# Input projection of a two-layer hybrid decoder: chunk pairs over all tokens by Strassen's seven products, and the layer in two phases

## The chip, the core and the metric

The program runs on one core of one Trainium2 chip. The time is device microseconds of one execution. TensorE (PE) multiplies, VectorE (DVE) and ScalarE (ACT) do elementwise work, GpSimd (POOL) and SyncE (SP) mostly issue DMAs; each engine works through its own queue in order. Matrix products write to PSUM, in banks of 128 partitions x 512 float32 columns.

## The reference

Two layers over 1024 tokens of width 1024. In each layer a conditioning vector gives a shift, a scale and a gate, and one wide projection feeds three token mixers:

```python
u    = x * (1.0 + scale) + shift
proj = u @ w_in                      # (1024 tokens, 7840 columns)
# A: a1 * sigmoid(a2) -> causal depthwise conv of 31 taps -> LayerNorm -> silu, times silu(a_gate), @ w_a_out
# B: gb * conv3(gc * xb), times silu(b_gate), @ w_b_out
# C: attention of 8 heads with low-rank q and kv and a rotary part, times silu(c_gate), @ w_c_out
m    = sum(sigmoid(merge_i) * y_i for i in range(3))
x    = layer_norm(alpha * x + gate * (m @ w_o))
```

Everything is float32.

## The kernel before

Data lie with features on the 128 partitions and tokens along the columns. The program works in four windows: two layers, and in each the tokens 0 to 511 and 512 to 1023. A product keeps float32 precision by splitting each operand into two float32r parts (`split`: the high part by ACT, the low part by DVE) and adding three passes, high x high, high x low and low x high (L131 to L133). The columns of w_in make 61 chunks of 128; a chunk of a window is 8 row blocks x 3 passes = 24 matmuls into one of three PSUM banks of the tag "pj". Its weights come as two units of 128x512: SP loads one, ACT and DVE split it (L81, L82). This happens anew in each window. `run` loads the units LOOKAHEAD = 3 ahead.

The order of the work is a list of jobs in `build`, woven by hand (`weave` spreads one list evenly behind another); each engine's queue follows from it through the tile framework's scheduler, and waits between engines are put in by that framework. In a window come the latent chunks for attention (5), branch A's eight chunks, the up-projections, then the chunks of B, the gates and the first merge logits, woven with the attention (per head and block of 128 queries: scores into one two-bank PSUM tile, DVE's maximum at L673, ACT's exponential at L675, transposes at L691, values at L707). The 31 convolution steps on DVE (L521, 128x512 each, two channel blocks per job) are woven into the same stretch. Then follow the other merges and the product with w_o, and the layer norm of a window lies in the head of the next.

A merge logit is a chunk whose tanh (L756) is used at once. Branch outputs stay in SBUF. Between the windows only a few carried columns are copied on POOL (L499, L502, L602, L605), and q, k and v go through DRAM by DMAs of POOL's queue. POOL's only arithmetic on two tiles is at the very end (L888). The conditioning's weighted sums (L230) are on DVE.

## Time and profile before

| | |
|---|---|
| time, median of 3 runs (lowest, highest) | 2230.21 us (2229.93, 2230.97) |
| the profiled execution, first to last instruction | 2231.9 us |
| matmuls | 10635 |
| DMA traffic | 313.79 MB, mean 141 GB/s |
| window-wise loads of w_in | 488 of 256 KB |

The profile records one execution, from its first to its last instruction; what lies around that span is not in it, and the profiled execution's own time is taken as its span. Busy time of an engine is the union of its instructions. Matmuls overlap in the records (a 512-column one lasts 0.39 us there and the next starts before it ends), so their pace is read from the starts. "A <- B" names who ended a wait.

### The profile page before, as it was taken

The numbers are of one execution on the slowest core, as the hardware profiler recorded it, in microseconds if no ns is written. First come the engines' busy times: TensorE is split into PE (matmuls) and PEld (weight loads), VectorE is DVE, ScalarE is ACT, GpSimd is POOL, SyncE is SP. The second block draws the span as 40 slices with busy tenths as digits, with TensorE's granted clock in tenths as the row PEclk, the third lists the DMA queues.
The fourth block names the chain that finished last, engine by engine and source line by source line (L and its number), as shares of the span: only waits on it lengthen the run. The fifth ranks groups of instructions, "written<-read, shape, count | busy, mean of one in ns | idle before, by whom it ended". The sixth has DMA issues, their size and how long they took to land.

```text
span 2231.9 us, 30546 instructions
## 1 busy us (share of the span) xinstructions
PE 2188.0 (98%) x10635; PEld 1809.1 (81%) x10635; DVE 1680.6 (75%) x2899; ACT 1072.3 (48%) x1915; POOL 222.8 (10%) x443
## 2 busy tenths in 40 slices
PE   6999999999999999999999999999999999999995
PEld 5788888888888888888888888888888888888885
DVE  7999955667999976576689996465579999556555
ACT  3644453444636555343464445443455555554343
POOL 0121100000121210000003111000002121100000
PEclk9999999999999999999999999999999999999998
DMA  8584443345594564345549443233448655322331
GB/s 291 183 234 114 112 126 94 95 133 193 161 278 109 128 140 126 117 131 162 161 137 289 131 119 100 85 95 95 139 135 260 165 123 121 94 76 87 103 124 60
DMA packets 177066, 313.79 MB, mean 141 GB/s; under 512 B 19600, under 2 KB 51856, under 8 KB 176912
## 3 DMA queue, kind: packets, MB, share of 16 engines
q1 hardware_dynamic: 130640, 231.60, 34.0%
q0 software_dynamic: 46272, 80.24, 14.3%
q8 instruction: 84, 1.38, 0.3%
q14 instruction: 70, 0.57, 0.1%
HBM read 271.39 MB, written 40.37 MB: 140 GB/s over the span
## 4 chain that ended last, share of the span: by engine, by line
PE 85%; issue 10%; DVE 2%; ACT 1%; DMA 0%; POOL 0%; SPq 0%; POOLq 0%; ACTq 0%; DVEq 0%
PE lgps L131 7%; PE lgps L133 7%; PE lgps L132 7%; PE avps L707 3%; PE yps L131 3%; PE yps L133 3%; PE yps L132 3%; PE tps L691 3%; PE ops L132 2%; PE ops L131 2%; PE ops L133 2%; PE score L668 2%; PE score L669 2%; PE score L670 2%; PE latps L131 1%
## 5 line engine op out<-in xcount | busy, mean ns | idle before, releaser
L82 DVE TENSOR_TENSOR wsplit<-wraw,wsplit 128x512 fp32r<-128x512 f32 (+1 forms) x692 | 471.4, 683 | 239.0 <-ACT wsplit L81 235.6
L81 ACT CAST wsplit<-wraw 128x512 fp32r<-128x512 f32 (+1 forms) x692 | 424.8, 615 | 460.4 <-PE lgps L133 82.9
L521 DVE SCALAR_TENSOR_TENSOR cacc<-abuf,vec,cacc 128x512 f32<-128x512 f32 x480 | 341.9, 744 | 0.1
L131 PE MATMUL lgps<-u,wsplit 128*128 128x512 f32 x768 | 307.4, 400 | 0.0
L133 PE MATMUL lgps<-u,wsplit 128*128 128x512 f32 x768 | 300.0, 391 | 0.0
L132 PE MATMUL lgps<-u,wsplit 128*128 128x512 f32 x768 | 299.8, 390 | 0.0
L133 PEld LDWEIGHTS lgps<-u,wsplit 128*128 128x128 f32 x768 | 144.2, 188 | 31.1
L131 PEld LDWEIGHTS lgps<-u,wsplit 128*128 128x128 f32 x768 | 144.7, 188 | 27.1 <-issue 1.0
L132 PEld LDWEIGHTS lgps<-u,wsplit 128*128 128x128 f32 x768 | 144.5, 188 | 27.2 <-issue 1.0
L675 ACT ACTIVATE prob<-score,nm 128x384 f32<-128x384 f32 (+7 forms) x128 | 95.1, 743 | 124.8 <-DVE nm L673 117.2
L82 DVE TENSOR_TENSOR pt<-tps,pt 128x512 fp32r<-128x512 f32 (+1 forms) x160 | 101.5, 634 | 48.1 <-ACT pt L81 47.0
L756 ACT ACTIVATE mt<-lgps 128x512 f32<-128x512 f32 x96 | 57.4, 597 | 150.0 <-PE lgps L133 150.0
L81 ACT CAST pt<-tps 128x512 fp32r<-128x512 f32 (+1 forms) x160 | 86.4, 540 | 70.5 <-PE avps L707 61.4
L131 PE MATMUL ops<-m,wsplit 128*128 128x512 f32 (+1 forms) x320 | 111.2, 348 | 0.1
L132 PE MATMUL ops<-m,wsplit 128*128 128x512 f32 (+1 forms) x320 | 110.9, 347 | 0.0
L133 PE MATMUL ops<-m,wsplit 128*128 128x512 f32 (+1 forms) x320 | 110.7, 347 | 0.0
L673 DVE TENSOR_REDUCE nm<-score 128x1 f32<-128x384 f32 (+7 forms) x128 | 96.4, 753 | 15.5 <-PE score L671 14.4
L677 ACT ACTIVATE prob<-prob,nm 128x384 f32<-128x384 f32 (+7 forms) x128 | 99.5, 778 | 15.3 <-DVE nm L676 15.2
L707 PE MATMUL avps<-pt,Vh 128*128 128x256 f32 x640 | 104.9, 286 | 0.0
L707 PEld LDWEIGHTS avps<-pt,Vh 128*128 128x128 f32 x640 | 95.3, 189 | 10.4
L691 PE MATMUL tps<-cs,prob 128*128 128x128 f32 x576 | 89.7, 272 | 0.0
L691 PEld LDWEIGHTS tps<-cs,prob 128*128 128x128 f32 x576 | 71.9, 140 | 18.2
(306 smaller groups left out, 5029.3 us busy)
## 6 DMA issues: line engine op xcount, KB each, us to landing
wraw<-in_win SPq DMA_DIRECT2D x488, 256.0 KB, 2.7
wraw<-in_wout SPq DMA_DIRECT2D x96, 256.0 KB, 2.6
adaraw<-in_wada SPq DMA_DIRECT2D x64, 256.0 KB, 3.3
wraw<-in_wo SPq DMA_DIRECT2D x64, 256.0 KB, 2.8
Kh<-knD POOLq DMA_DIRECT2D x48, 256.0 KB, 4.7
Vh<-vD POOLq DMA_DIRECT2D x48, 256.0 KB, 4.1
adaraw<-in_wada SPq DMA_DIRECT2D x16, 512.0 KB, 6.7
knD<-knope POOLq DMA_DIRECT2D x16, 512.0 KB, 4.9
```

Source lines behind the costliest of these rows:

```text
L81: nc.scalar.copy(dst[:, 0], src)
L82: nc.vector.tensor_tensor(dst[:, 1], src, dst[:, 0].bitcast(F32), op=ALU.subtract)
L131: mm(ps, w[:, 0, c], x[k][:, 0, cols], start=k == 0, stop=False)
L132: mm(ps, w[:, 0, c], x[k][:, 1, cols], start=False, stop=False)
L133: mm(ps, w[:, 1, c], x[k][:, 0, cols], start=False, stop=k == 4 * len(units) - 1)
L521: nc.vector.scalar_tensor_tensor(acc, a[:, k:k + T], w, acc, op0=ALU.mult, op1=ALU.add)
L673: nc.vector.tensor_reduce(nm[:, 0:1], sp[:, :nk], axis=AX.X, op=ALU.max, negate=True)
L675: nc.scalar.activation(p[:, :nk], sp[:, :nk], AF.Exp, bias=nm[:, 0:1], accum_out=nm[:, 1:2])
L677: nc.scalar.mul(p[:, :nk], p[:, :nk], nm[:, 2:3])
L691: nc.tensor.transpose(tp[:, c:c + P], st["p", hd, 2 * half + b][:, (2 * kp + k) * P:(2 * kp + k + 1) * P], self.ident)
L707: mm(av[:, half * 256:(half + 1) * 256], v[:, 2 * kp + k], pt[:, w, (1 - k) * 256:(2 - k) * 256], start=kp == 0 and k == 0 and w == 0, sto ...
L756: nc.scalar.activation(st["t"], ps, AF.Tanh, scale=0.5)
```

## The change

56 of the 61 chunks are now computed in pairs, for all 1024 tokens at once. A pair is a 2x2 block product: two chunks by two halves of the 1024 input features, times two halves of the features by two halves of the tokens. Strassen's scheme (in Winograd's form) takes seven block products where eight stood. The factors on the side of u (X11, X12, X22 and the sums S1 to S4) are built once a layer and kept split in SBUF (`s_job`); those on the side of w_in are built for each pair by four subtractions on POOL (`pair_units`), and all seven factors are split by ACT and DVE. Each product adds into one of the three banks (A and C take two products, B three), and the sums across banks are made by one copy on ACT and five additions on DVE, which read the bank between two products (`pair_jobs`). The even row blocks of w_in come first in DRAM (KO). The latents (5 chunks) stay as they were.

A layer has two phases. The first computes the latents and up-projections for both halves of the tokens, then all 28 pairs: 12 of merge logits, 4 of A (a2, a1), 8 of B, 2 of C's gates and 2 of A's gates. The convolution runs over 1024 columns at a time, one channel block per job, woven into 12 of these pairs. The tanh of the logits, C's gates and the split branch outputs of A and B go to DRAM (by ACT's, POOL's and POOL's queue). The second phase does, for each half of the tokens, the merges with B and A woven with the attention (for the second half also w_o and the norm of the first), then the merges with C; logits are loaded on SP and branch outputs on POOL. SBUF tiles have fixed homes that serve several uses (HOMES).

```diff
-LOOKAHEAD = 3
-UPW = 20
-# bounds of the first units of weights, loaded behind each early block of the conditioning
-SP = (0, 3, 7, 10, 14)
+LOOKAHEAD = 5
+KO = (0, 2, 4, 6, 1, 3, 5, 7)
+SP = (0, 3, 6, 8, 10)
...
+    "X11": homes(0, 4), "S2": homes(4, 8), "S1": homes(8, 12), "X12": homes(12, 16), "S3": homes(16, 20),
+    "S4": homes(20, 24), "X22": homes(24, 28), "X21": ["c0", "c1", "c2", "c3"],
...
+    def pair_units(self, l, c1, c2):
+        nc = self.nc
+        st = {}
+        def raw(key, c, half):
+            st[key] = self.pw.tile([P, T], F32, tag="wr", name="wraw")
+            nc.sync.dma_start(st[key], self.win[l, c, :, half * T:(half + 1) * T])
+        def part(t):
+            w = self.pw.tile([P, 2, T], F32R, tag="ws", name="wsplit")
+            self.split(w, t)
+            return w
+        def minus(d, a, b):
+            nc.gpsimd.tensor_tensor(d, a, b, op=ALU.subtract)
+        def w11():
+            for key, c, half in (("11", c1, 0), ("12", c2, 0), ("22", c2, 1), ("21", c1, 1)):
+                raw(key, c, half)
+            return part(st["11"])
+        def t2():
+            minus(st["11"], st["12"], st["11"])
+            st["t2"] = self.pw.tile([P, T], F32, tag="tt", name="wt")
+            minus(st["t2"], st["22"], st["11"])
+            return part(st["t2"])
+        def t3():
+            minus(st["12"], st["22"], st["12"])
+            return part(st["12"])
+        def t4():
+            minus(st["t2"], st["21"], st["t2"])
+            return part(st["t2"])
+        return [w11, t2, lambda: part(st["11"]), lambda: part(st["21"]), t3, lambda: part(st["22"]), t4]
...
+    def pair_jobs(self, l, c1, c2, post, name):
+        nc = self.nc
+        st = {}
+        add = lambda d, a, b: nc.vector.tensor_tensor(d, a, b, op=ALU.add)
+        def tmp(key):
+            st[key] = self.t2("w", key)
+            return st[key]
+        def p1():
+            nc.scalar.copy(tmp("a1"), st["A"])
+        def p6():
+            add(tmp("a2"), st["a1"], st["B"])
+        def p5():
+            add(tmp("a5"), st["a1"], st["C"])
+        def p2():
+            post(0, 0, st["A"])
+        def p7():
+            add(st["a5"], st["a5"], st["B"])
+            post(1, 1, st["a5"])
+        def p3():
+            add(st["a2"], st["a2"], st["C"])
+            post(1, 0, st["a2"])
+        def p4():
+            add(st["a1"], st["a1"], st["B"])
+            post(0, 1, st["a1"])
+        steps = [("X11", "A", p1), ("S2", "B", p6), ("S1", "C", p5), ("X12", "A", p2), ("S3", "B", p7),
+                 ("S4", "C", p3), ("X22", "B", p4)]
+        units = self.pair_units(l, c1, c2)
+        def part(n, half):
+            key, b, end = steps[n]
+            def fn(ws):
+                if half == 0:
+                    st["w"] = ws[0]
+                    if n < 3:
+                        st[b] = self.bank(name, "pj")
+                w, ps = st["w"], st[b]
+                mm = nc.tensor.matmul
+                for k in (2 * half, 2 * half + 1):
+                    x = self.state[key, l][k]
+                    c = slice(k * P, (k + 1) * P)
+                    for i, (a, e) in enumerate(((0, 0), (0, 1), (1, 0))):
+                        mm(ps, w[:, a, c], x[:, e], start=n < 3 and k == 0 and i == 0, stop=k == 3 and i == 2,
+                           skip_group_check=True)
+                if half:
+                    end()
+            return ([] if half else [units[n]], fn)
+        return [part(n, half) for n in range(7) for half in range(2)]
...
+    def s_job(self, l, i):
+        nc = self.nc
+        x11, x12, x21, x22 = (self.affine(l, h, 2 * i + e, act=True) for h in range(2) for e in range(2))
+        tt = nc.vector.tensor_tensor
+        tt(x11, x11, x21, op=ALU.subtract)
+        self.factor(l, "S3", x11)
+        tt(x21, x21, x22, op=ALU.add)
+        self.factor(l, "S1", x21)
+        tt(x22, x22, x11, op=ALU.subtract)
+        self.factor(l, "S2", x22)
+        tt(x12, x12, x22, op=ALU.subtract)
+        self.factor(l, "S4", x12)
...
-    def conv_jobs(self, l, j0):
+                nc.scalar.activation(t, t, AF.Tanh, scale=0.5)
+                glu(1, t, st["v"])
+        return self.pair_jobs(l, CH_A2 + j, CH_A1 + j, post, "aps")
+    def conv_jobs(self, l, j):
         nc = self.nc
 
         def step(k):
             def fn(_):
-                for j in (j0, j0 + 1):
-                    w = self.vec[l][:, V_CAW + j * 31 + k:V_CAW + j * 31 + k + 1]
-                    a = self.state["abuf", j]
-                    if k == 0:
-                        acc = self.pt.tile([P, T + 30], F32, tag="ab", name="cacc")[:, :T]
-                        self.state["cacc", j] = acc
-                        nc.vector.tensor_scalar(acc, a[:, 0:T], w, self.vec[l][:, V_CAB + j:V_CAB + j + 1],
-                                                op0=ALU.mult, op1=ALU.add)
-                    else:
-                        acc = self.state["cacc", j]
-                        nc.vector.scalar_tensor_tensor(acc, a[:, k:k + T], w, acc, op0=ALU.mult, op1=ALU.add)
+                w = self.vec[l][:, V_CAW + j * 31 + k:V_CAW + j * 31 + k + 1]
+                a = self.state["abuf", j]
+                if k == 0:
+                    acc = self.pa.tile([P, S], F32, tag=f"c{j}", name="cacc")
+                    self.state["cacc", j] = acc
+                    nc.vector.tensor_scalar(acc, a[:, 0:S], w, self.vec[l][:, V_CAB + j:V_CAB + j + 1],
+                                            op0=ALU.mult, op1=ALU.add)
+                else:
+                    acc = self.state["cacc", j]
+                    nc.vector.scalar_tensor_tensor(acc, a[:, k:k + S], w, acc, op0=ALU.mult, op1=ALU.add)
...
+    def keep(self, key, t, scale):
+        p = self.pair("sp", "yp")
+        self.split(p, t, scale)
+        d = self.pd.tile([P, 2, T], F32R, name="y" + "".join(map(str, key)))
+        self.nc.gpsimd.dma_start(d, p)
+        self.state[("yD",) + key] = d
...
+    def logit_pair(self, l, n, d0):
+        nc = self.nc
+        def post(i, h, t):
+            key = ("tD", l, n, d0 + i)
+            if key not in self.state:
+                self.state[key] = self.pd.tile([P, S], F32, name=f"tD{l}{n}{d0 + i}")
+            m = self.t2("w", "mt") if (i, h) == (0, 0) else t
+            nc.scalar.activation(m, t, AF.Tanh, scale=0.5)
+            nc.scalar.dma_start(self.state[key][:, h * T:(h + 1) * T], m)
+        return self.pair_jobs(l, CH_M + 3 * d0 + n, CH_M + 3 * d0 + 3 + n, post, "lgps")
...
-        def logit(ps):
-            st["t"] = self.t2("m", "mt")
-            nc.scalar.activation(st["t"], ps, AF.Tanh, scale=0.5)
+        def logit(_):
+            st["t"] = self.t2("w", "mt")
+            nc.sync.dma_start(st["t"], self.state["tD", l, n, d][:, h * T:(h + 1) * T])
...
+            jobs += weave(part0, side0, 0, len(part0))
+            lat1, up1 = self.head(l, 1)
+            jobs += weave(lat1, [([], lambda _, l=l, i=i: self.s_job(l, i)) for i in range(4)], 2, len(lat1) - 2)
+            lg = [self.logit_pair(l, n, 2 * i) for n in range(3) for i in range(4)]
+            body = weave(lg[0] + lg[1], up1, 0, 28)
+            convs = [self.conv_jobs(l, j) for j in range(4)]
+            fill = [lg[2] + lg[3] + lg[4], lg[5] + lg[6] + lg[7], lg[8] + lg[9] + lg[10],
+                    lg[11] + self.cg_pair(l, 0) + self.cg_pair(l, 2)]
             for j in range(4):
-                fill += self.b_jobs(l, h, j)
-                if j % 2 == 0:
-                    fill += self.cg_job(l, h, j // 2)
-            for d in range(8):
-                fill += self.merge_jobs(l, h, "B", d)
-                if d % 4 == 1:
-                    fill += self.cg_job(l, h, 2 + d // 4)
-            body = weave(fill, self.att_jobs(l, h), 8, len(fill))
-            for d in range(8):
-                body += self.merge_jobs(l, h, "C", d)
-            lna = self.lna_jobs(l)
-            body = weave(body, self.conv_jobs(l, 0) + self.conv_jobs(l, 2) + lna[:2], 0, len(body) - 28)
-            body = weave(body, lna[2:], len(body) - 24, len(body) - 10)
-            tail = [j for k in range(4) for j in self.ag_job(l, h, k)]
-            for d in range(8):
-                tail += self.merge_jobs(l, h, "A", d)
-            last = w + 1 == len(wins)
+                body += self.a_pair(l, j) + weave(fill[j], convs[j], 0, len(fill[j]))
+            tail = [x for j in range(4) for x in self.b_pairs(l, j)]
+            lna = self.lna_jobs(l, 0) + self.lna_jobs(l, 1)
+            body += weave(tail, lna, 20, len(tail) - 14)
+            body += self.ag_pair(l, 0) + self.ag_pair(l, 2)
+            if l == 0:
+                body = weave(body, adas, 40, len(body) - 40)
+            jobs += body
+            for h in range(2):
+                ab = self.y_jobs(l, h, "B")
+                for d in range(8):
+                    ab += self.merge_jobs(l, h, "B", d)
+                ab += self.y_jobs(l, h, "A")
+                for d in range(8):
+                    ab += self.merge_jobs(l, h, "A", d)
+                if h:
+                    wo = [j for e in range(8) for j in self.wo_jobs(l, 0, e)]
+                    ab = wo + self.ln_jobs(l, 0) + ab
+                body = weave(ab, self.att_jobs(l, h), 0, len(ab) - 6)
+                for d in range(8):
+                    body += self.merge_jobs(l, h, "C", d)
+                jobs += body
```

## Rows read from the trace of the kernel before

**Rows 1.** The page: busy us (share of the span) and instructions of three engines.

```profile
span 2231.9 us, 30546 instructions
PE 2188.0 (98%) x10635; PEld 1809.1 (81%) x10635; DVE 1680.6 (75%) x2899; ACT 1072.3 (48%) x1915; POOL 222.8 (10%) x443
```

**Rows 2.** The page: the chain that ended last, shares by engine.

```profile
PE 85%; issue 10%; DVE 2%; ACT 1%; DMA 0%; POOL 0%; SPq 0%; POOLq 0%; ACTq 0%; DVEq 0%
```

**Rows 3.** Waits of PE: us in total, times, longest us.

```profile
PE adaps L238 <- DVE adacc L230: 14.9, 3, 11.6
```

**Rows 4.** Timeline of PE, 51 products in a row: start us, us.

```profile
400.21 0.39 PE L131 MATMUL lgps<-u,wsplit 128*128 128x512 f32 x1
...
411.55 0.39 PE L133 MATMUL lgps<-u,wsplit 128*128 128x512 f32 x1
```

**Rows 5.** Busy us (instructions) by stretch, then granted clock, DMA share, GB/s.

```profile
core 0: us, PE busy (x) PEld busy (x) DVE busy (x) ACT busy (x) POOL busy (x), PEclk, DMA share, GB/s
120.00:180.00 60.00, 60.00 (x280) 48.72 (x280) 58.82 (x104) 27.27 (x57) 16.21 (x33) 1.00 0.68 192
```

**Rows 6.** Timeline of DVE.

```profile
1327.92 0.75 DVE L521 SCALAR_TENSOR_TENSOR cacc<-abuf,vec,cacc 128x512 f32<-128x512 f32 x1
1328.58 0.69 DVE L603 TENSOR_TENSOR pbuf<-gcps,xb 128x512 f32<-128x512 f32 x1
1329.18 0.68 DVE L82 TENSOR_TENSOR wsplit<-wraw,wsplit 128x512 fp32r<-128x512 f32 x1
1329.78 0.48 DVE L608 TENSOR_SCALAR cvb<-pbuf,vec 128x512 f32<-128x512 f32 x1
```

**Rows 7.** DVE's groups by shape: busy us, mean ns | idle before.

```profile
L673 DVE TENSOR_REDUCE nm<-score 128x1 f32<-128x1024 f32 x16 | 19.6, 1222 | 4.0 <-PE score L671 3.5
...
L673 DVE TENSOR_REDUCE nm<-score 128x1 f32<-128x512 f32 x16 | 11.0, 686 | 1.1 <-PE score L671 1.0
...
L673 DVE TENSOR_REDUCE nm<-score 128x1 f32<-128x128 f32 x16 | 4.6, 286 | 0.7 <-PE score L671 0.7
```

**Rows 8.** Line 888: duration ns min/median/max, first and last start us.

```profile
L888 DVE TENSOR_TENSOR r<-r,emr x5: 411/420/504, 2218.1 to 2221.2; 128x256 f32<-128x256 f32 x5
...
L888 POOL TENSOR_TENSOR r<-r,emr x3: 723/727/781, 2218.4 to 2222.0; 128x256 f32<-128x256 f32 x3
L888 POOLq MODIFY_POOL_CONFIG  x2: 1/3/5, 2002.4 to 2002.4; - x2
```

**Rows 9.** Timeline near the end, DVE and POOL.

```profile
2220.30 0.72 POOL L888 TENSOR_TENSOR r<-r,emr 128x256 f32<-128x256 f32 x1 [1.16 <-DVE r L887]
2220.80 0.84 DVE L888 TENSOR_TENSOR r<-r,emr 128x256 f32<-128x256 f32 x2
```

**Rows 10.** Line 602, a copy of two columns on POOL.

```profile
L602 POOL COPY pbuf<-carryB x8: 185/197/634, 496.7 to 1830.4; 128x2 f32<-128x2 f32 x8
```

**Rows 11.** Timeline of POOL beside rows 6.

```profile
1329.33 0.58 POOL L605 COPY carryB<-pbuf 128x2 f32<-128x2 f32 x1 [5.50 <-DVE pbuf L603]
```

**Rows 12.** Busy us of a tile's own instructions: transposes, values, scores of one window.

```profile
140.00:360.00 220.00, 12.65 (x80) 10.22 (x80) 14.36 (x24) 12.33 (x24) 1.00 0.44 120
...
140.00:360.00 220.00, 15.25 (x96) 14.69 (x96) 5.46 (x8) 4.65 (x8) 1.00 0.44 120
...
140.00:360.00 220.00, 23.31 (x128) 16.67 (x96) 15.54 (x32) 19.81 (x64) 1.00 0.44 120
```

**Rows 13.** ACT's groups by shape.

```profile
L675 ACT ACTIVATION_READ_ACCUMULATOR prob<-score,nm 128x1 f32 x128 | 24.7, 193 | 0.0
...
L675 ACT ACTIVATE prob<-score,nm 128x512 f32<-128x512 f32 x16 | 11.0, 689 | 17.9 <-DVE nm L673 17.9
...
L675 ACT ACTIVATE prob<-score,nm 128x128 f32<-128x128 f32 x16 | 5.9, 368 | 11.5 <-DVE nm L673 11.5
```

**Rows 14.** Busy us of the start.

```profile
0.00:48.00 48.00, 28.89 (x125) 23.06 (x125) 35.33 (x67) 17.60 (x28) 0.30 (x5) 0.98 0.86 303
```

More of the change, by code (lines that the diff above doesn't have):

```diff
@@ L113, in run, with chunk @@
             fn(loaded[done - len(us):done])
[L115 removed]
+    def chunk(self, units, xs, post, name, tag="pj", cols=slice(0, T), kept=None, where=lambda k: (k // 4, k % 4)):
         st = {}
         kept = {} if kept is None else kept
[L119 removed]
+        again = "planned" in kept
+        kept["planned"] = True
+        n = 4 * len(units)
+        loaded = set()
         def part(i):
+            new = [] if again else sorted({where(k)[0] for k in (2 * i, 2 * i + 1)} - loaded)
+            loaded.update(new)
             def fn(ws):
@@ L137, in chunk @@
-        jobs = [part(i) for i in range(2 * len(units))]
-        kept.setdefault("planned", True)
-        return jobs
+            return ([units[u] for u in new], fn)
+        return [part(i) for i in range(n // 2)]
     def in_chunk(self, l, h, ch, post, name, tag="pj"):
         return self.chunk([self.win[l, ch, :, 0:T], self.win[l, ch, :, T:2 * T]],
-                          lambda: self.state["u", l, h], post, name, tag)
+                          lambda: self.state["u", l, h], post, name, tag, where=lambda k: (k % 2, k // 2))
@@ L916, in build @@
                         self.setup()
-                    for k in order[SP[n]:SP[n + 1]]:
-                        first[k] = self.load_w(units[k], "ws" if k < 4 else "br" if k < 12 else "PT")
+                    for k in range(SP[n], SP[n + 1]):
+                        first.append(self.load_w((units[k], HOMES["first"][k])))
                     self.u_job(0, 0, 2 * n)
@@ L970, in build @@
-            jobs += head + body + tail + wo
-            prev = (l, h)
-        jobs.append(([], lambda _: self.end_jobs(*prev, slice(T // 2, T))))
+                    part = [j for e in range(8) for j in self.wo_jobs(l, 1, e, c, tags[2 * e:2 * e + 2], kept[e])]
+                    jobs += weave(part, self.ln_jobs(l, 1, slice(0, T // 2)), 2, 30) if c.start else part
+        jobs.append(([], lambda _: self.end_jobs(L - 1, 1, slice(T // 2, T))))
         self.run(jobs, first)
```

366 lines of the change are left out of this document (185 added, 181 removed).

## The prediction, made before the changed kernel ran

> **What bounds the kernel now.** I read the page's busy shares first, then the chain that ended last, then what TensorE waited for, then single stretches of TensorE and DVE. TensorE is busy for 2188.0 of 2231.9 us, VectorE (DVE) for 1680.6, and ScalarE (ACT) for 1072.3 [rows 1]. The chain is 85% TensorE and 10% "issue", which is the same stream of matmuls [rows 2]. What it waits for most is the conditioning at the start, 14.9 us [rows 3]. So time is the number of matmuls times their pace: 400.21 to 411.55 us holds 50 steps, 0.2268 us for each 512-column matmul [rows 4]. DVE is second, and not evenly so: while the 31-tap convolution runs it is busy 58.82 of 60 us, and TensorE, at a granted clock of 1.00 (the 2.4 GHz level), still loses nothing there [rows 5], because the work that it waits for is spread over three PSUM banks of 5.4 us each (24 x 0.2268).
>
> **What the change removes.** 56 of the 61 chunks of w_in are taken in pairs. A pair over both halves of the tokens cost 2 x 2 x 24 = 96 matmuls and now costs 7 x 4 x 3 = 84. 28 pairs a layer, 2 layers: 56 x 12 = 672 matmuls, 672 x 0.2268 = **152.4 us** off TensorE [rows 4]. The 2 x 7 x 4 x 3 passes themselves have the old shape, so I keep the old pace. Nothing else in TensorE's work changes. Beneath this, 2231.9 - 152.4 = 2079.5, it cannot go.
>
> **What it adds on DVE, and where.** Costs from start to start: a two-input operation on 512 columns 0.60 us (1328.58 to 1329.18), a convolution step 0.66 (1327.92 to 1328.58) [rows 6]. On 1024 columns: the reductions cost 686 ns at 512 and 1222 at 1024, 0.536 for 512 more columns [rows 7], so a step becomes 0.66 + 0.536 = 1.20 us where there were two of 0.66; 240 wide steps save 240 x 0.12 = 29 us. A pair needs 7 low parts of split weights instead of 8, and 5 new additions that read a PSUM bank: 12 x 0.60 = 7.2 us against 4.8. Over 56 pairs that is +134 us. The factor sums of u (s_job) add 64 operations, 38 us. DVE as a whole goes from 1681 to about 1820 of 2080 us.
>
> The sum hides where it lies. Each layer's projection phase has 560 us of TensorE work and all of the convolution, but the convolution is woven only into 12 of the 28 pairs (fill[0] to fill[3], three pairs each, 31 steps per three). There a pair costs DVE 7.2 + 31/3 x 1.20 = 19.6 us; TensorE needs 84 x 0.2268 = 19.05. In layer 0 the rest of the conditioning (8 blocks of 8 steps at 0.66, 42 us) is woven over the same jobs, 1.6 us a pair: 21.2. And the cover is thinner: product 5 goes into bank B and product 7 needs B again one product later, so B's addition has 2.7 us (12 x 0.2268) to happen; the same from product 7 to the next pair's second. DVE's lag is passed on to TensorE almost at once. In these 24 pairs DVE sets the pace: 12 x 0.55 + 12 x 2.15 = **+32 us**.
>
> **POOL's subtractions.** GpSimd (POOL) gets 4 a pair, 224 in all, 128x512 from SBUF; before has three of 128x256, 727 ns [rows 8]. A two-column copy takes 185 when nothing is in its way [rows 10], so (727 - 185)/254 per column gives about 1.27 us for 512. That alone is 5 us of POOL per 19 us, hidden behind the five units of weights (13.6 us) by which loads run ahead. The question is what it does to DVE. The copies show the two in each other's way: the same two columns take 185 ns or up to 634 [rows 10], and a slow one, from 1329.33 for 0.58 us [rows 11], ends just behind a low part (two SBUF inputs) that DVE ran from 1329.18 to 1329.86 [rows 6]. The other direction shows once: of five DVE subtractions of 256 columns, one took 504 ns against 411 to 420 [rows 8], and it is the one that started at 2220.80 while POOL's ran from 2220.30 to 2221.02 [rows 9]; it got going about when POOL stopped reading. I take from this that one holds the other off for its whole reading, about 1.1 us per subtraction. In the woven pairs 17 of 22 DVE operations read two SBUF tiles (low parts, convolution); the 5 additions read PSUM and can run beside it. That leaves about 0.9 us a subtraction, 3.6 a pair. Bounds: 0 (behind the slow copy DVE's next operations start on time, 1329.18 to 1329.78 [rows 6]) to 4 x 1.27 = 5.1 a pair. 24 pairs x 3.6 = **+87 us** (0 to 122); a gain is excluded, there is no such work before. In the other 32 pairs DVE has 8 to 16 us of work in 19, so 3.6 more is absorbed; I take 0 there, up to +15.
>
> The Trainium skill, SBUF — State Buffer, "Who interferes with whom", says that a DVE instruction with two SBUF inputs and a GpSimd instruction that reads SBUF exclude each other and that the second fully blocks. By it the 87 us stand; by the copy alone, which delayed no DVE operation, the term would be 0. The single 504 ns row agrees with the rule.
>
> **The heads of the layers.** The latents and up-projections used to share DVE with 8 chunks of branch A on TensorE; these have moved out. For tokens 0 to 511 TensorE has (120 + 16 + 102) x 0.2268 = 54 us; I count 108 DVE operations' worth of 0.60 in layer 1 (norm of the layer before, u, splits, two root-mean-square norms), 65 us, and 115, 69 us, in layer 0 (rotary tables instead of the norm). For tokens 512 to 1023: 136 matmuls, 31 us, against 60 operations, 36 us. Excess 11 + 5 and 15 + 5 = 36; some of it can run on into the up-projections behind, so **+30 us** (0 to 60).
>
> **The second phase.** Attention keeps its work but loses its filler: it ran over some 200 us of projection chunks per window; now, for the first half, over 192 output matmuls (43.5 us) and its own 51 us [rows 12], for the second over 384 (87 us) and, from twice to three times as many keys, an estimated 98. One score buffer serves: scores, reduction, exponential, then the next. Bare, in the first half: 0.6 us of TensorE, the reduction (0.286 to 0.686, mean 0.49) [rows 7], the exponential (0.368 to 0.689, mean 0.53) and its 0.19 accumulator read [rows 13]: 1.8 us x 32 = 58 of some 90 us. With an operation of 0.6 queued ahead on each of DVE and ACT, 3.0 x 32 = 96. So I take 8 us a layer for the first half, 7 for the second: **+30**. At the change of phase q, k, v and the branch outputs come back through DRAM into buffers that the last pair frees late; the loads are issued on POOL, 4 of 512 KB, with little to run meanwhile: **+5** a layer, **+10** (0 to 80 together with attention).
>
> **Small terms.** At the start five chunks instead of seven are loaded, whole rather than by first halves; TensorE did 125 matmuls in the first 48 us [rows 14], 32 of them the conditioning's and 93 projection; by the units at hand in each of the four blocks I count 72 that can be done by then, 21 x 0.2268 less: **+5**. ACT gets 56 copies and 96 DMA issues and loses 56 casts; with 1072 of 2232 busy it hides them. Logits, gates and branch outputs add 92 MB of DRAM traffic, weights lose 57; queues stand well below full. The logits' loads sit on SP among the weights, six slots ahead: 0.
>
> **Sum.** 2231.9 - 152.4 + 32 + 87 + 30 + 30 + 10 + 5 = 2273.5. The median of the runs shown, 2230.21, lies 1.7 below the profiled span, so the forecast is **2272 us**: slower by 1.9%.
>
> **Rivals.** (a) POOL does not hold DVE up: its reading falls between DVE's, at the subtractions in the 24 woven pairs. Price -87: 2185 us, faster. It decides as soon as a subtraction costs DVE less than 0.47 us (the sum reaches 2230 when the 87 shrink to 45, and 45/96 = 0.47). For it: the copy delayed no DVE operation. Against it: the 504 ns row, and that the long ones can't fit in a gap of 0.1 us. (b) TensorE stays the bound throughout, as in [rows 5]: DVE's order of work lets lag build up and be made good later. 2231.9 - 152.4 + 5 - 1.7 = 2083. Against it: the one product that bank B leaves DVE, and 103 to 111% of DVE in the woven pairs even without POOL. (c) The single score buffer sets the pace of the second phase: two operations ahead of each step instead of one, 4.2 x 32 = 134 against 90 in the first half, 5.8 x 32 = 186 against 185 in the second; 45 a layer instead of 15, +60 on the forecast, and with late loads about 2340. (d) POOL changes its program: an instruction of that name stands before its first subtraction and nowhere else [rows 8], hidden in 216 us of idleness. If it came back whenever POOL turns from issuing DMAs to subtracting, weights would be late; no row gives a price, it lies above (c).
>
> **How the numbers follow.** Forecast 0.54, with its own range 2235 to 2325. (a) 0.27, 2140 to 2225. (b) 0.06. (c) and (d) together 0.10. Between, within 0.2% (what a measurement of this kernel can tell): 0.03. Faster: 0.27 + 0.06 + 0.03 from the forecast's lower tail = 0.36; same 0.04; slower 0.60. The range that leaves out (b), the lower end of (a), and (d): 2150 to 2345.
>
> **What would show it.** Right: TensorE's wait list led by projection matmuls waiting for DVE's additions and low parts, DVE at 9 in the slices of the convolution, DVE operations with two SBUF inputs well above 687 ns on average where POOL subtracts, while the additions from PSUM stay near 0.68. (a) shows as the same operations at 687 ns; (b) as TensorE at full throughout; (c) as score matmuls waiting for exponentials; (d) as repeated program changes on POOL. The matmul count must fall by 672 at 0.227 us a step; if the pace of the products differs, the first term is wrong. The forecast fails if the woven pairs run at 19 us.

## The result, and the profile after

The kernel after takes **2466.57 us** (median of 4 runs, 2462.88 to 2469.21) against 2230.51: ratio 1.1057, 95% interval 1.1041 to 1.1073. Slower, as forecast, but by 10.6% where 1.9% was said and 2345 us was the end of the range. Runs of one kernel differ by up to 11 us here (e12), and most experiments have a single run; a smaller difference is given below as a number, but decides nothing.

The page's span, busy shares and chain, which answer to [rows 1, 2]:

```profile
span 2465.8 us, 29700 instructions
PE 2173.3 (88%) x9963; PEld 1744.1 (71%) x9963; DVE 1918.4 (78%) x2915; ACT 1091.0 (44%) x1954; POOL 609.4 (25%) x715
...
PE 33%; issue 33%; DVE 13%; POOL 12%; DMA 5%; ACT 4%; POOLq 0%; ACTq 0%; SPq 0%; DVEq 0%
```

The 672 matmuls are gone (10635 to 9963), yet TensorE's busy time fell by 15 us and not by 152, and it idles for 293 us where it idled for 44. Busy time grew without matmuls where the granted clock was low: 280 matmuls of the first logit pairs took 73.36 us at 0.86 (fourth row below), 285 of them 66.07 at 1.00 in e2. By stretch (us from the span's start, then busy us and count of each engine, granted clock, DMA share, GB/s): the start, which answers to [rows 14]; latents and up-projections of the first half, of the second, the first two logit pairs; the same three in layer 1; then the first and second half of phase 2 in layer 0, the second in three parts.

```profile
0.00:48.00 48.00, 29.51 (x104) 22.31 (x104) 34.71 (x67) 15.13 (x24) 0.20 (x4) 0.89 0.86 308
48.00:148.00 100.00, 56.00 (x185) 40.08 (x186) 73.03 (x140) 44.94 (x78) 11.00 (x20) 0.69 0.53 169
148.00:188.00 40.00, 35.57 (x145) 27.87 (x145) 24.09 (x36) 21.64 (x36) 8.31 (x7) 0.88 0.50 157
188.00:285.00 97.00, 73.36 (x280) 55.73 (x281) 60.00 (x100) 47.14 (x83) 16.96 (x23) 0.86 0.48 153
1273.00:1359.00 86.00, 66.34 (x270) 48.56 (x268) 68.61 (x127) 46.21 (x83) 10.77 (x20) 0.92 0.61 193
1359.00:1397.00 38.00, 33.92 (x146) 26.93 (x147) 24.03 (x37) 20.84 (x36) 8.32 (x7) 0.96 0.49 154
1397.00:1491.00 94.00, 71.05 (x279) 53.40 (x279) 58.90 (x99) 46.11 (x81) 16.92 (x22) 0.89 0.51 160
...
872.00:1002.00 130.00, 117.64 (x593) 92.76 (x592) 89.35 (x180) 73.65 (x167) 43.94 (x88) 0.93 0.97 230
...
1002.00:1077.00 75.00, 74.69 (x401) 61.21 (x400) 48.02 (x79) 46.66 (x82) 16.11 (x32) 1.00 0.69 168
1077.00:1130.00 53.00, 40.46 (x201) 32.69 (x200) 38.61 (x68) 35.01 (x58) 12.18 (x24) 0.81 0.59 182
1130.00:1230.00 100.00, 99.68 (x548) 82.96 (x547) 77.52 (x128) 59.63 (x102) 13.92 (x27) 1.00 0.60 156
```

In the second row no engine is full: TensorE 56, VectorE 73 of 100 us, and 0.69 of the clock, between its levels of 1.2 and 2.4 GHz. Such a stretch is a chain of waits, not a load. TensorE's waits, the first rows of the list (engine, line, releaser, total, times, longest):

```profile
PE lgps L264 <- DVE a L217: 43.1, 19, 4.3
PE score L841 <- ACT prob L848: 33.2, 26, 5.2
PE rstd L488 <- DVE rsrow L458: 27.6, 4, 16.7
PE adaps L362 <- DVE adacc L354: 26.3, 8, 11.3
PE lgps L264 <- ACT sq L502: 24.4, 4, 11.6
```

The first is the one foretold, products waiting for VectorE's additions; the third belongs to the heads (longest 16.7 us), the fifth to the factor sums (11.6 us; it is gone in e2). Of the fourth, 14.9 us lie at the start, as before. The subtractions on POOL (line, count, ns min/median/max), and VectorE's groups in 285 to 653 us, layer 0's branch-A and woven pairs:

```profile
L191 POOL TENSOR_TENSOR wraw<-wraw x112: 1272/1300/2526, 166.7 to 2010.8; 128x512 f32<-128x512 f32 x112
L191 POOL TENSOR_TENSOR wt<-wraw x56: 1268/1616/2162, 168.5 to 2008.6; 128x512 f32<-128x512 f32 x56
L191 POOL TENSOR_TENSOR wt<-wraw,wt x56: 1262/1652/2268, 174.3 to 2012.7; 128x512 f32<-128x512 f32 x56
```

```profile
L670 DVE SCALAR_TENSOR_TENSOR cacc<-abuf,vec,cacc 128x1024 f32<-128x1024 f32 x115 | 152.3, 1325 | 0.1
L107 DVE TENSOR_TENSOR wsplit<-wraw,wsplit 128x512 fp32r<-128x512 f32 x76 | 58.8, 776 | 4.8 <-ACT wsplit L106 4.8
L354 DVE SCALAR_TENSOR_TENSOR adacc<-adaraw,cact,adacc 128x512 f32<-128x512 f32 x41 | 42.5, 1036 | 0.0
L217 DVE TENSOR_TENSOR a<-a,lgps 128x512 f32<-128x512 f32 x50 | 33.9, 678 | 5.5 <-PE lgps L264 5.5
```

Alone a subtraction takes 1.26 us, as worked out (1.27); low parts rose from 683 to 776 ns, the conditioning's steps from 750 to 1036; the additions from PSUM are at 678, and at 675 in e5 without any subtraction. How the two engines meet, in layer 1 (start us, us, what; idle before in brackets):

```profile
1647.60 1.28 DVE L670 SCALAR_TENSOR_TENSOR cacc<-abuf,vec,cacc 128x1024 f32<-128x1024 f32 x1
1647.76 2.27 POOL L191 TENSOR_TENSOR wraw<-wraw 128x512 f32<-128x512 f32 x1 [13.52 <-DVE wsplit L107]
1648.80 0.68 DVE L217 TENSOR_TENSOR a<-a,lgps 128x512 f32<-128x512 f32 x1
1649.39 1.72 DVE L670 SCALAR_TENSOR_TENSOR cacc<-abuf,vec,cacc 128x1024 f32<-128x1024 f32 x1
1650.11 2.15 POOL L191 TENSOR_TENSOR wt<-wraw 128x512 f32<-128x512 f32 x1
...
1652.29 0.62 ACT L106 CAST wsplit<-wt 128x512 fp32r<-128x512 f32 x1 [5.33 <-POOL wt L191]
...
1652.95 1.12 DVE L107 TENSOR_TENSOR wsplit<-wt,wsplit 128x512 fp32r<-128x512 f32 x1 [1.83 <-ACT wsplit L106]
```

Whoever came first kept the other out. POOL's first subtraction ends at 1650.03, 1.15 us after the convolution step that was there before it (1648.88); the addition, with one operand in PSUM, passed untouched; the next step, from 1649.39, ends 1.08 us after POOL's end; POOL's second one 1.15 us after that step. The trace repeats this with hardly any scatter: 31 convolution steps that met a subtraction under way end 1.08 to 1.09 us after it, 80 low parts 0.55 to 0.56. Behind them ScalarE stood 5.33 us for the difference.

### The profile page after: what moved, and what is told of

Its sections match the earlier page's. It is cut to its first block, busy times and chain, and to the rows that moved or that the text cites. A ratio compares the mean times of both kernels' runs of the same rounds, so it can differ in the third digit from the quotient of the medians.

```text
span 2465.8 us, 29700 instructions
## 1 busy us (share of the span) xinstructions
PE 2173.3 (88%) x9963; PEld 1744.1 (71%) x9963; DVE 1918.4 (78%) x2915; ACT 1091.0 (44%) x1954; POOL 609.4 (25%) x715
## 4 chain that ended last, share of the span: by engine, by line
PE 33%; issue 33%; DVE 13%; POOL 12%; DMA 5%; ACT 4%; POOLq 0%; ACTq 0%; SPq 0%; DVEq 0%
POOL wt L191 5%; POOL wraw L191 5%; PE avps L880 3%; DVE wsplit L107 3%; PE yps L163 2%; PE yps L164 2%; PE yps L165 2%; PE agps L264 2%; PE tps L864 2%; PE score L841 2%; PE lgps L264 2%; PE bgps L264 2%; PE ops L163 1%; DVE cacc L670 1%; PE ops L165 1%
## 5 line engine op out<-in xcount | busy, mean ns | idle before, releaser
L264 PE MATMUL lgps<-u,wsplit 128*128 128x512 f32 x2016 | 502.3, 409 | 81.5 <-DVE a L217 43.1
L106 ACT CAST wsplit<-wraw 128x512 fp32r<-128x512 f32 (+1 forms) x524 | 316.9, 614 | 296.8 <-PE yps L165 55.0
L670 DVE SCALAR_TENSOR_TENSOR cacc<-abuf,vec,cacc 128x1024 f32<-128x1024 f32 x240 | 321.6, 1340 | 0.3
L191 POOL TENSOR_TENSOR wraw<-wraw 128x512 f32<-128x512 f32 x112 | 182.0, 1625 | 536.9 <-DVE wsplit L107 536.7
L264 PE MATMUL xgps<-u,wsplit 128*128 128x512 f32 x672 | 160.9, 396 | 12.2 <-DVE a L217 12.1
L264 PE MATMUL bgps<-u,wsplit 128*128 128x512 f32 x672 | 159.2, 393 | 6.5 <-DVE a L217 6.5
L264 PE MATMUL aps<-u,wsplit 128*128 128x512 f32 x672 | 157.6, 394 | 5.6 <-DVE a L217 3.0
L264 PEld LDWEIGHTS xgps<-u,wsplit 128*128 128x128 f32 x672 | 126.2, 189 | 44.3 <-DVE a L217 12.5
L264 PEld LDWEIGHTS aps<-u,wsplit 128*128 128x128 f32 x672 | 127.1, 190 | 34.6 <-DVE qnope L110 4.3
L264 PEld LDWEIGHTS bgps<-u,wsplit 128*128 128x128 f32 x672 | 125.1, 188 | 37.1 <-DVE a L217 9.5
```

Source lines behind the costliest of these rows:

```text
L106: nc.scalar.copy(dst[:, 0], src)
L191: nc.gpsimd.tensor_tensor(d, a, b, op=ALU.subtract)
L264: mm(ps, w[:, a, c], x[:, e], start=n < 3 and k == 0 and i == 0, stop=k == 3 and i == 2, skip_group_check=True)
L670: nc.vector.scalar_tensor_tensor(acc, a[:, k:k + S], w, acc, op0=ALU.mult, op1=ALU.add)
```

## The experiments

Stretches of both layers together, in us, from the first matmul of one tile name to that of the next (e4, e13 and e14 have another order, so take their first two columns as one sum). The first 15 us, the 43 us between the layers and the last 69 us are in no column. The last row is the matmul count times 0.2268 [rows 4], for phase 2 TensorE's busy time times its granted clock.

| kernel | time | heads | first 2 logit pairs | 32 A and woven pairs | 20 later pairs | phase 2, first halves | second halves |
|---|---|---|---|---|---|---|---|
| after | 2466.6 | 297 | 190 | 710 | 426 | 260 | 455 |
| e1 bare | 2330.1 | 290 | 186 | 618 | 390 | 262 | 454 |
| e2 no sums | 2389.0 | 293 | 141 | 709 | 425 | 235 | 457 |
| e3 eighth | 2575.5 | 297 | 205 | 777 | 449 | 260 | 457 |
| e4 heads | 2417.7 | 357 | 82 | 701 | 430 | 264 | 453 |
| e5 no subtr. | 2335.2 | 287 | 188 | 616 | 400 | 265 | 450 |
| e6 half conv | 2417.3 | 299 | 190 | 672 | 410 | 263 | 453 |
| e13 free | 2241.9 | 337 | 80 | 613 | 400 | 231 | 453 |
| e14 on DVE | 2320.7 | 346 | 81 | 652 | 412 | 261 | 433 |
| e15 residual | 2446.3 | 295 | 188 | 709 | 427 | 262 | 435 |
| e16 3 fills | 2341.8 | 285 | 190 | 618 | 403 | 261 | 456 |
| e17 unused | 2439.1 | 291 | 195 | 686 | 424 | 259 | 455 |
| matmuls alone | | 170 and the start | 122 | 610 | 381 | 219 | 412 |

**e1, without Strassen's subtractions and additions.**

```diff
-            add(tmp("a2"), st["a1"], st["B"])
+            nc.scalar.copy(tmp("a2"), st["B"])
...
-            minus(st["12"], st["22"], st["12"])
```

> Leaves out the 168 subtractions of weights on GpSimd and the 280 additions of products on VectorE (two of the sums per pair become ScalarE copies, so that every result is still stored); the factor sums stay. Theory 1, exposed latency in front of the pairs and in the attention: only the excess inside the woven and the unwoven pairs goes (about 106 us in the 32 pairs at 22.4 us, up to 38 us in the unwoven ones), and the heads (100 and 86 us) and the stretch of the factor sums (97 and 94 us) stay within 15 us of what they are: 2330 to 2390 us. Theory 2, the arithmetic of Strassen on VectorE and GpSimd sets the pace throughout, as the prediction had it: with it gone the time falls to 2100 to 2220 us and the stretch of the factor sums falls by over 40 us.

2330.12 us. (The subtractions are 224, four a pair; 168 is a slip of that text.) The 32 pairs fall to TensorE's pace (618 us against 610), and nothing before or behind the pairs moves by more than 7: theory 1.

**e2, without the factor sums.**

```diff
-        x11, x12, x21, x22 = (self.affine(l, h, 2 * i + e, act=True) ...
+        for s, x in (("S1", "X11"), ("S2", "X12"), ("S3", "X22"), ("S4", "X12")):
+            self.state[s, l] = self.state[x, l]
```

> Leaves out the factor sums of the tokens: S1 to S4 are taken to be the X tiles that are there already, so 32 loads, 32 affine steps, 32 sums and 32 splits go. Theory 1 (the sums are a serial chain that the first logit pairs wait for): the two stretches of the first logit pairs fall from 97 and 94 us towards 61, the second heads a little too, 55 to 80 us in all: 2385 to 2415 us. Theory 2 (pace of VectorE and GpSimd): these stretches are not short of VectorE time, so 2445 to 2470 us.

2388.95 us, 78 less: 50 in the stretches of the first logit pairs, as theory 1 has it, and 25 where nobody expected them, in the first halves of phase 2. Both rows of e2, which stand against 97.00 and 130.00 above:

```profile
184.00:256.00 72.00, 66.07 (x285) 51.16 (x284) 45.28 (x77) 32.55 (x60) 16.95 (x23) 1.00 0.56 183
838.00:953.00 115.00, 110.41 (x595) 86.66 (x594) 88.02 (x178) 72.33 (x165) 38.71 (x79) 1.00 1.03 234
```

The chain of waits after, in layer 1, shows the sums as a file: load, affine on ScalarE, sums and low parts on VectorE, then the next load, held by the six temporaries.

```profile
1395.12 2.98 DMA xu<-xD
1398.13 0.82 ACT xu L421
1398.98 0.70 DVE xu L445
...
1402.28 3.11 DMA xu<-xD
1405.47 0.82 ACT xu L421
...
1412.91 3.08 DMA xu<-xD
```

The 25 us: attention's keys, values and branch outputs are loaded into the places of S1 to S4, which the last pair frees late; in e2 these stood empty. That is read from the places, not tried by itself.

**e3, the fourth product twice.**

```diff
+                    if n == 3:
+                        for i, (a, e) in enumerate(((0, 0), (0, 1), (1, 0))):
+                            mm(ps, w[:, a, c], x[:, e], start=False, ...)
```

> Issues the fourth product of every pair a second time, 672 more matmuls, as many as the change took away; the sums come out with that product twice. If TensorE sets the pace of the pairs: 672 x 0.2268 = 152 us more, 2619 us. Theory 1 and 2 both have the 32 woven pairs bound by VectorE (22.4 us against 19.05 + 2.72 = 21.8 us of matmuls), so only the 24 unwoven pairs pay, 24 x 2.72 = 65 us: 2500 to 2540 us. If nothing is bound by TensorE any more: 2465 to 2480 us.

2575.47 us, +109: a miss for all three. The 32 pairs that were held to be VectorE's pay 67 of their 87 us, the later 20 only 23 of 54. So in the woven pairs TensorE's work and the waits add up; VectorE does not run ahead as a bound of its own.

**e4, heads filled.**

```diff
-                part0 = lat0 + up0
+                part0 = lat0
-            jobs += weave(lat1, [... s_job ...], 2, len(lat1) - 2)
+            jobs += weave(lat1, up0, 0, len(lat1))
+            jobs += weave(up1, [... s_job ...], 0, len(up1))
-            body = weave(lg[0] + lg[1], up1, 0, 28)
+            body = lg[0] + lg[1]
```

> Same computation, other order: the latents of the first half, then those of the second half with the up-projections of the first half between them, then the up-projections of the second half with the factor sums between them, then the first two logit pairs. Theory 1 (the heads lack matmuls beside their chains, and the low granted clock follows): the second head's chains find filler and the factor sums come ahead of the pairs, 50 to 110 us less: 2355 to 2415 us. Theory 2: no unit of VectorE or GpSimd work changes, 2450 to 2470 us. If the factor sums, now in a shorter stretch, make the up-projections late: above 2470 us.

2417.66 us: 49 from order alone, theory 1, just short of its 50 to 110.

**e5, without the subtractions** (the second edit of e1 alone)**; e6, 16 of 31 convolution steps.**

```diff
-        return [step(k) for k in range(31)]
+        return [step(k) for k in range(0, 31, 2)]
```

> Leaves out GpSimd's 168 subtractions of weights alone (each product takes a weight block that is there already); the additions stay. The prediction's term, 0.9 us of VectorE held off per subtraction: 87 us go in the woven pairs, 2365 to 2385 us. Rival, from the trace after (VectorE's neighbours of a subtraction are stretched by some 0.4 us each): 96 x 0.4 = 38 us in the woven pairs and up to 20 us elsewhere, the additions being the larger part of what went when both were left out: 2405 to 2435 us.

> Leaves out 15 of the 31 steps of every causal convolution, 120 steps x 1.34 us = 161 us of VectorE time in the woven pairs, and nothing else. If VectorE's load sets the pace of the woven pairs: the stretch of the 16 A and woven pairs falls as far as it did without Strassen's arithmetic (369 to 313 and 342 to 305 us), 93 us in all, 2365 to 2385 us. If the pairs wait for GpSimd's weights or for the latency of the additions: less than 40 us, 2425 to 2465 us.

e5: 2335.24 us. Nearly all that e1 gained is the subtractions', 131 us; the 280 additions cost 5, within the scatter. Both numbers of the expectation were too small. e6: 2417.28 us, between its two ranges; 120 steps less give the 32 pairs 38 us, so VectorE's load is not the whole of it. VectorE's groups in e5, the same work as above (278 to 591 us):

```profile
L665 DVE SCALAR_TENSOR_TENSOR cacc<-abuf,vec,cacc 128x1024 f32<-128x1024 f32 x115 | 146.5, 1274 | 0.1
L107 DVE TENSOR_TENSOR wsplit<-wraw,wsplit 128x512 fp32r<-128x512 f32 x108 | 73.0, 681 | 5.7 <-ACT wsplit L106 5.7
L212 DVE TENSOR_TENSOR a<-a,lgps 128x512 f32<-128x512 f32 x50 | 33.8, 675 | 0.5 <-PE lgps L259 0.5
L349 DVE SCALAR_TENSOR_TENSOR adacc<-adaraw,cact,adacc 128x512 f32<-128x512 f32 x41 | 30.4, 741 | 0.2 <-DMA adaraw<-in_wada 0.2
```

The low parts are back at the 683 ns of the kernel before, the conditioning's steps at its 750. Three woven pairs and the branch-A pair behind them in e5, then the same three woven pairs in the kernel after:

```profile
298.00:356.00 58.00, 58.00 (x262) 48.13 (x261) 57.09 (x70) 20.02 (x34) 0.00 (x0) 1.00 0.41 135
356.00:376.00 20.00, 19.92 (x88) 16.18 (x87) 18.00 (x26) 7.14 (x12) 0.12 (x1) 1.00 0.41 137
305.00:376.00 71.00, 63.61 (x261) 51.42 (x259) 65.66 (x71) 20.62 (x36) 22.78 (x12) 0.93 0.32 107
```

In e5 VectorE is nearly full in the woven pairs and TensorE loses nothing; 4 of the convolution's 31 steps run on into the branch-A pair. With 12 subtractions the same work takes some 13 us longer. Over all 24 woven pairs the subtractions cost some 89 us, 0.9 each.

**e7, two score buffers in the first halves; e8, no logit loads.**

```diff
+                if h == 0 and qb % 2:
+                    sp = self.bank("score")
...
-            nc.sync.dma_start(st["t"], self.state["tD", l, n, d][:, h * T:(h + 1) * T])
+            st["t"] = self.ones.unsqueeze(1).to_broadcast([P, 4, P])
```

> Same computation; in the first half's attention every other score tile takes a bank of the projection's three, so that scores alternate between two buffers. If the single score buffer sets the pace of the first halves of phase 2 (130 and 131 us, of which TensorE is busy 118): 8 to 12 us each, 2440 to 2452 us. If the DMA engines do (they are busy 0.97 of these stretches): within 5 us, 2460 to 2470 us.

> Leaves out the loading of the merge logits in phase 2 (96 loads of 256 KB; a constant takes their place). If the DMA engines set the pace of the first halves of phase 2, busy 0.97 at 230 GB/s: 12.6 of some 60 MB go there, 10 to 20 us each, 2425 to 2450 us. If the single score buffer does: within 8 us, 2458 to 2470 us.

2464.42 and 2466.18 us: neither. The first halves take 263 and 256 us against 260, so neither the single score buffer nor the DMA share of 0.97 is shown to set the pace there. The bank that e7 gives to the scores is taken from the merges, though, which could hide a gain; that was not tried apart.

**Contention or order? e9, e10, e16, e17.** e9 issues three subtractions of a pair behind its first split and splits their results later; e10 and e16 fill the tile two or three times; e17 subtracts into a tile that nobody reads:

```diff
             w = part(st["11"])                          # e9
+            minus(st["11"], st["12"], st["11"])
+            minus(st["t2"], st["22"], st["11"])
+            minus(st["12"], st["22"], st["12"])
...
-            nc.gpsimd.tensor_tensor(d, a, b, op=ALU.subtract)
+            for _ in range(3):                          # e16; e10: 2
+                nc.gpsimd.memset(d, 0.03)
...
-            minus(st["12"], st["22"], st["12"])
+            minus(st["t2"], st["22"], st["12"])         # e17, t2 unused
```

> Same computation, the same 224 subtractions (four a pair; the count of 168 in two earlier expectations was wrong): three of a pair's four are issued on GpSimd right behind the first split, the fourth two units ahead, and the splits that read their results one or two units (2.7 us each) later than now. Theory A, order: ScalarE, which works in order, stands at the rounding of a difference that GpSimd has not finished (296 us in the trace after, none of it with other work to pass it), and what is queued behind it, the copies of products out of the banks, is late: most of the 131 us that the subtractions cost comes back, 2340 to 2395 us. Theory B, contention, as predicted: GpSimd's reading holds VectorE off (its neighbours are stretched, the convolution step from 1.28 to 1.72 us): the time stays, 2440 to 2465 us.

> In place of each subtraction GpSimd writes the same tile twice with a constant: it keeps its place in the chain of waits and about the same time (two fills of 512 columns against 1.3 to 1.6 us), but reads nothing from SBUF; the weights of three products are constants. Theory A (order): ScalarE still waits for GpSimd, a little shorter: 2400 to 2450 us. Theory B (contention): the price goes with the reading, 2335 to 2365 us.

> As e10, with three fills in place of each subtraction: 3 x 0.52 = 1.57 us, the 1.6 us that a subtraction took, so that GpSimd is as long in the chain as it was, and still reads nothing. e10 left ScalarE 114 us of waiting for GpSimd where there were 296, so it had shortened the order's wait as well. Theory A (order; ScalarE and what is queued behind it stand while GpSimd is at work): 2390 to 2450 us. Theory B (contention): 2335 to 2360 us.

> The 224 subtractions run on GpSimd with the same operands as reads, but their results go to a tile that nobody uses, and the products take the loaded weights as in e5: the contention without the wait of ScalarE for GpSimd. Theory A (order): 2335 to 2365 us. Theory B (contention): at least the 89 us by which VectorE's recorded time is longer, 2420 to 2465 us. Between, both have a part, and the two runs divide the 131 us.

2460.66, 2338.59, 2341.81 and 2439.13 us. e9 decides nothing by itself: ScalarE's wait for POOL stayed, as the first row, from e9, shows. The others do: occupation without reading costs 3 to 7 us over e5, within the scatter (e16 keeps 165 of ScalarE's 296 us of waiting), reading without the wait 104.

```profile
ACT wsplit L106 <- POOL wt L194: 299.0, 52, 12.0
```

```profile
ACT wsplit L106 <- POOL wt L192: 96.2, 27, 8.4
ACT wsplit L106 <- POOL wraw L192: 68.7, 34, 5.4
```

```profile
L107 DVE TENSOR_TENSOR wsplit<-wraw,wsplit 128x512 fp32r<-128x512 f32 (+1 forms) x636 | 490.7, 776 | 76.7 <-ACT wsplit L106 74.2 <-PE latps L165 1.6
L670 DVE SCALAR_TENSOR_TENSOR cacc<-abuf,vec,cacc 128x1024 f32<-128x1024 f32 x240 | 342.9, 1429 | 0.3
```

The last two rows are e17's: low parts at 776 ns, convolution at 1429, with no engine waiting for a difference. So it is POOL's reading that costs. How the 131 us divide between the contention itself and the waits that it lengthens is not settled: against e5, low parts, convolution and conditioning's steps together are 112 us longer in e17 but only 82 in the kernel after, so 104 is rather too much for its contention alone.

**e11, norm spread over the merges; e15, residual loaded at the start of its chunk.**

```diff
-                    ab = wo + self.ln_jobs(l, 0) + ab
+                    ab = wo + weave(ab, self.ln_jobs(l, 0), 0, len(ab) - 8)
...
+        def fetch(_):
+            pre["x"] = self.t2("x", "xr", n)
+            nc.sync.dma_start(pre["x"], self.x_src(l, h, e)[:, cols])
...
+        return [([], fetch)] + self.chunk(...)
```

> Same computation; in the second half of phase 2 the 12 steps of the first half's layer norm are spread over the merges of the branches B and A instead of standing in a row ahead of them. If the attention's excess there is lack of matmuls beside the norm (the 53 us from 1077 have 40 us of TensorE at a granted clock of 0.81): 10 to 18 us a layer, 2430 to 2448 us. If it is the single score buffer: within 6 us, 2460 to 2470 us.

> Same computation; each load of the residual x for the output projection is issued at the start of its chunk instead of in the step that needs it at once. If ScalarE, which stands at that load (7.8 us at 1079) with the attention's exponentials queued behind, is what opens the hole in the second halves of phase 2 (53 us from 1077 with 40 us of TensorE): 8 to 25 us less, 2440 to 2458 us. If the hole comes from the chain of norm and exponentials itself: 2460 to 2470 us.

2464.50 us: not the norm. 2446.32 us: 20 less, all in the second halves. The chain after, at the hole from 1077, had named it:

```profile
1079.15 7.81 DMA xr<-in_xT
1087.04 0.63 ACT xr L967
1087.67 0.89 ACT prob L848 x2
1088.60 0.80 PE score L841
```

A load issued in the step that needs it; ScalarE, in order, stands at it, and the exponentials queue behind. With the load early (e15) the hole shrinks from 53 to 43 us:

```profile
1072.00:1115.00 43.00, 37.23 (x185) 29.91 (x184) 35.45 (x64) 33.41 (x55) 12.54 (x24) 0.84 0.76 211
```

**Together: e12 (e4, e9, e11), e14 (e4, e9, e15 and the line below), e13 (e2, e4, e5).**

```diff
-            nc.gpsimd.tensor_tensor(d, a, b, op=ALU.subtract)
+            nc.vector.tensor_tensor(d, a, b, op=ALU.subtract)
```

> Same computation; the head order of e4, the early subtractions of e9 and the spread norm of e11 together. If the three causes lie in different stretches, the gains add: 49 + what e9 and e11 give; with theory A 2230 to 2320 us, with theory B 2380 to 2415 us. Not faster than the kernel before by more than 0.5% in either.

> Same computation as e12 without the spread norm, with the 224 subtractions on VectorE instead of GpSimd, and the residual's loads of e15. VectorE gets 224 x 0.68 = 152 us more, and loses what GpSimd's reading added (131 us by e5, 128 by e10). In the 16 A and woven pairs of a layer it then has 296 + 44 = 340 us (layer 0) and 268 + 44 = 312 us, against 305 of TensorE: +35 and +7 there, up to 20 elsewhere. 2409 - 131 + 60 = 2340 us, 2315 to 2385 us. If VectorE pays its 152 us in full: 2420 to 2440 us.

> Leaves out the subtractions of weights and the factor sums of the tokens, in the head order of e4: the seven products, the additions and the two phases with everything that Strassen's factors cost taken away. If the prices found so far lie in different stretches they add: 2335.2 - 77.6 - 48.9 = 2209 us; if the head order only gains what the missing sums gain anyway, 2258 us. So 2205 to 2260 us, at most 1% faster than the kernel before and 125 us and more above the 2080 us that the matmuls alone need: the rest is then the two-phase structure (heads and attention). If instead Strassen's factors are the whole loss: below 2150 us.

e12: 2409.31 us, 1.0809 of before (1.0790 to 1.0827); 8 less than e4 alone, within the scatter. e14, the best version that computes everything: 2320.74 us, 1.0409 (1.0391 to 1.0428). VectorE does the subtractions at 683 ns, and its other work runs undisturbed:

```profile
L681 DVE SCALAR_TENSOR_TENSOR cacc<-abuf,vec,cacc 128x1024 f32<-128x1024 f32 x114 | 145.4, 1276 | 0.0
...
L194 DVE TENSOR_TENSOR wraw<-wraw 128x512 f32<-128x512 f32 x32 | 21.9, 683 | 0.0
```

e13: 2241.94 us, 1.0051 (1.0036 to 1.0066). With both sets of factors for nothing, 672 matmuls fewer still do not beat the kernel before: the two-phase order, with the additions that are left, costs what they save. The time lies 33 us above the plain sum of the three gains, because they overlap in the heads: heads and first logit pairs take 417 us here, still 125 above their matmuls.

## Why the prediction was wrong

- **Removed: right.** 672 matmuls, and where nothing stands in the way (e5, layer 1) 16 pairs take 302.6 us, 18.9 each, against 19.05 worked out.
- **VectorE's pace, +32: not there.** Without subtractions the 32 pairs take 616 us against 610 of matmuls, with all additions, and leaving these out as well gives 5 us, within the scatter. I had VectorE at 103 to 111% within the 24 woven pairs and let TensorE follow at once. VectorE is indeed full there (57.09 of 58 us in e5), but the lag is made good in the branch-A pairs between, which rival (b) said and I gave 0.06.
- **POOL's subtractions, +87: right for the 24 woven pairs, 131 in all.** There they cost some 89 us, 0.9 each, as worked out. The step that failed is the 0 (up to 15) for the rest: 6 us in the branch-A pairs, 26 in the 20 later pairs and 9 in the heads, some 42 together, 131/224 = 0.58 us a subtraction on average. I let the other pairs absorb them because VectorE had 8 to 16 us of work in 19 there; in e5 it has 17.8 a pair in the later pairs of layer 0 and 16.7 in layer 1. Rival (a) is out. The Trainium skill, SBUF — State Buffer, "Who interferes with whom", says that issue order decides who blocks and that a GpSimd instruction that only writes does not contend with VectorE's second input. The trace agrees with both, the first by the times from 1647.60 to 1652.26, the second by e16 (convolution steps at 1277 ns beside 672 fills, 1276 in e5).
- **Heads, +30: the step that weighs most.** I counted VectorE's operations against TensorE's matmuls as loads. In the first head of layer 0 neither was full (73 and 56 of 100 us, clock 0.69). What counted were chains with no matmuls beside them, and each matmul took longer at the lower clock. Heads and first logit pairs together take 487 us, 195 above their 292 of matmuls, the waits at the start included. Filling them by order takes off 48 (e4), the factor sums' part (next point) is 53 and the subtractions' 12, each tried alone. That the rest comes from the chains and the clock is read from the rows; no run shows it.
- **Factor sums, 38 us of VectorE, priced at nothing: 78 us.** Hidden work must be early; I never asked when it could start, and counted its 64 operations on VectorE but not the 32 loads of u in front of them. With six temporaries the four jobs run one behind the other, each behind a 3 us load, in front of the first product that needs them (50 us), and their tiles hold places that phase 2 wants (25, by the places, not tried by itself).
- **Second phase, +40: about 84,** the two halves together 715 us against 631. Of it 25 us come from late places (e2) and 20 from the residual's load (e15). The mechanism I named, the single score buffer, is not shown as a cause in the first halves (e7, 263 us against 260); in the second it wasn't tried. Some 40 us stay open, about half of them in each kind of half. (The first half's 43.5 + 51 us make 94.5, not the 90 that the sum used; that makes its excess smaller, not larger.)
- **(d) POOL's program** changed twice in all, before the first subtraction: out.
- **Start, +5: right.** TensorE did 104 matmuls in the first 48 us where it had done 125 [rows 14], the 21 fewer that I had counted.

That the two terms that I worked hardest on, 119 us for VectorE and POOL, came out near 131 + 5 is luck: one was not there, and the other was half as large again. So is the direction: by the sum it hung on POOL's term, without which it gave 2185 us, faster (rival (a)); without a subtraction the kernel still takes 2335 (e5). The rest of the 386 us above the floor (2465.8 - 2079.5), some 250, lies mostly in the heads, the factor sums and the second phase, for which, with the start, the sum had 75.

## What to carry to other kernels

A saving on the bounding engine is also a loss of filler: list every stretch that the moved matmuls used to cover, and price it as the chain that is left, at the clock that a waiting TensorE got there, not as busy shares. For work that "hides", ask when its inputs and its buffers are there. Before putting two-input element-wise work on GpSimd, see whether VectorE reads two SBUF tiles at that time: here VectorE itself was cheaper, at 0.68 us each (e14's 52 pairs take 48 us more than e5's, those of the kernel after 120).

## What the runs showed of the hardware

- Subtraction on POOL and two-input operations on VectorE exclude each other: the second ends 1.15 us (POOL, of 1.26), 1.08 (convolution step, of 1.28) or 0.55 (low part, of 0.68) after the first, so all but 0.1 to 0.2 us of it runs alone. Either can be the one that waits (POOL up to 2.53 us, a convolution step 1.72).
- POOL's fills (527 ns for 512 columns) left VectorE's two-input operations alone: its conditioning steps are at 745 ns beside 672 of them, 744 in e5. They did hold up steps with one SBUF input: the first step of each convolution (128x1024, L667) took 1522 ns on average in e16 against 812 in e5, once 2.64 us.
- Issuing a subtraction earlier changed nothing clear of the scatter while it wrote in place over a tile that VectorE had still to read (POOL idle behind VectorE's split for 554 us in e9, 570 without it).
- TensorE's granted clock was 0.69 where it was busy 56 of 100 us, 0.93 at 118 of 130 and 1.00 at 110 of 115 (e2).
